# Scaling odd tiles of x on GpSimd, and the modulation products ahead of the weights' low halves, in the first stage of a decoder trunk

## The chip, the core and the metric

One core of a Trainium2 chip runs the whole kernel. The metric is the device time of one execution in microseconds. Two matmul clocks occur on TensorE, 1.2 and 2.4 GHz; the profile gives the granted clock as a share of the higher one. Engines are called TensorE (PE), VectorE (DVE), ScalarE (ACT), GpSimd (POOL) and SyncE (SP, whose queue issues all loads and stores here).

## What is computed

The reference is a trunk of two layers on x (1024 tokens by 1024 channels) with a conditioning vector c: a Mamba-2 layer, then a stick-breaking attention layer over a shared K and V, each with a residual. Only its beginning matters here:

```python
c_act = jax.nn.silu(c)
shift, scale, gate = jnp.split(c_act @ ada_w[i] + ada_b[i], 3, axis=-1)
xf = xf * lax.rsqrt(jnp.mean(xf * xf, axis=-1, keepdims=True) + EPS)
h = (xf * g) * (1.0 + scale) + shift
zxbcdt = h @ in_w
```

So every token (row) of x is divided by its root mean square, every channel is scaled and shifted by numbers that come from a product of a vector (the silu of c) with a matrix (ada_w), and the result h is multiplied by the first projection.

## The kernel before

Matrix products run on float32 values split into a high part and a low part (fp32r): one product is three matmuls (`mm3`, lines 128 to 131: high by high, high weights by low values, low weights by high values).

**The first stage** (lines 158 to 342) is written out by hand: inside `manual_schedule` (line 172) the instructions of TensorE, ScalarE, GpSimd and VectorE run in the order of the code. Loads are issued by SP in the order of lines 179 to 193. Behind the first stage the order of all engines but TensorE in some stages comes from a planner with a simulated timeline (`schedule_with_timeline_sim=True`, line 1107).

The 1024 tokens lie in 8 tiles of 128 tokens by 1024 channels (`xn[t]`), in two halves of 4 tiles (`hf` 0 and 1). The channels are 8 blocks `d` of 128. The steps, each a small function:

- `squares(t)` (200) sums the squares of a tile's rows, on VectorE for t = 1, 3, 7, on ScalarE for the others. `rms(hf)` (214) makes the inverse roots of a half: two steps on ScalarE (139, 140) and three small **root steps** on VectorE (144 to 146).
- `scaled(t)` (217) multiplies a tile by its roots, in place: odd tiles on VectorE (220), even ones on ScalarE (222).
- `turn(d, hf)` (252) transposes block d of the four tiles of a half on TensorE into PSUM (`xp`). `spin` (210) issues filler matmuls whose results are not used.
- `gemv(d)` (224) makes shift and scale of block d: two **modulation products** on VectorE, each a product of a 128x1024 tile of `ada0` (`a`) with the silu of c (`crow`) with an accumulated sum. Line 296 prepares a small vector from the biases for all blocks. `bias(d)` (245) finishes both numbers on ScalarE.
- `split_w(d, V)` (230) splits the weights `ww` of block d: the high halves `wwh` are copied on ScalarE (233), the low halves `wwl` are subtracted on VectorE (234).
- `high(d, hf)` (258) applies scale and shift to `xp` (`hx`, line 260) and copies the high part `h0h` (263), both on ScalarE. `low(d, hf)` (266) subtracts the low part `h0l` on VectorE (268).
- `wave_mm(d, hf)` (270) accumulates three output tiles: nine matmuls, of which the second needs `h0l` and the third `wwl`.

The order is that of lines 280 to 341: squares, roots and scalings of the first half, two transposed blocks, fillers, weights and products of d = 0, then the wave of the first half; then roots and scalings of the second half, its transposes, and so on to d = 7. The loads of later blocks reuse buffers: `a0` has four, `ww` three.

Of the kernel before, what the change touches and what calls it, by code (L numbers as in the profile page):

```python
# [15 lines left out]
ALU = mybir.AluOpType  # L16
# [31 lines left out]
def f(ap):  # L48
    return ap.bitcast(F32)
# [3 lines left out]
def tile_trunk(ctx, tc, xT, xN, c, vec, ada0, adar, wxbc, wwave, wdt, wz, wmo, wk, wv, wq, wqz, wso, out):  # L53
    nc = tc.nc
    V, S, Q, E, Y = nc.vector, nc.scalar, nc.gpsimd, nc.tensor, nc.sync
# [14 lines left out]
    def vv(n, i=None, m=1):  # L70
        o, w = VEC[n]
        if i is None:
            return vt[:, o:o + w]
        return vt[:, o + i:o + i + m]
# [35 lines left out]
    def act_tile(name):  # L110
        return act.tile([P, HT], F32R, tag="a", name=name)

    def mm_tile(name):
        return pmm.tile([P, HT], F32, tag="mm", name=name)
# [43 lines left out]
    with ExitStack() as es:  # L158
# [14 lines left out]
        xn = [px.tile([P, D], F32, name=f"x{t}") for t in range(NC_)]  # L173
# [36 lines left out]
        def spin(x, m):  # L210
            for i in range(m):
                E.matmul(wave[NW - 1][:, HT:], ident, x, start=True, stop=True)
# [4 lines left out]
        def scaled(t):  # L217
            r = rst[:, t // CPH, t % CPH:t % CPH + 1]
            if t % 2:
                V.tensor_scalar(out=xn[t], in0=xn[t], scalar1=r, scalar2=None, op0=ALU.mult)  # L220
            else:
                S.activation(xn[t], xn[t], AF.Identity, scale=r)

        def gemv(d):
            for i, m in enumerate((SH0, SC0)):
                a = a0s[d][:, i, :]
                V.scalar_tensor_tensor(out=a, in0=a, scalar=1.0, in1=crow, op0=ALU.mult, op1=ALU.mult,
                                       accum_out=mod[:, m, d:d + 1])

        def split_w(d, eng):  # L230
            wh = pada.tile([P, NW, P], F32R, tag="wwh", name=f"wwh{d}", bufs=4)
            wl = pada.tile([P, NW, P], F32R, tag="wwl", name=f"wwl{d}", bufs=4)
            S.copy(wh, wws[d])
            eng.tensor_tensor(out=wl, in0=wws[d], in1=f(wh), op=ALU.subtract)
            whl[d] = wh, wl
# [16 lines left out]
        def turn(d, hf):  # L252
            ps = mm_tile(f"xp{d}_{hf}")
            for i in range(CPH):
                E.transpose(ps[:, i * P:(i + 1) * P], xn[hf * CPH + i][:, d * P:(d + 1) * P], ident)
            xps[d, hf] = ps

        def high(d, hf):
            hx = tp.tile([P, HT], F32, tag="hx", name=f"hx0_{d}_{hf}", bufs=3)
            S.activation(hx, xps.pop((d, hf)), AF.Identity, bias=mod[:, SH0, d:d + 1],  # L260
                         scale=mod[:, SC0, d:d + 1])
            h0[d][hf] = (act_tile(f"h0h{d}_{hf}"), act_tile(f"h0l{d}_{hf}"))
            S.copy(h0[d][hf][0], hx)
            hxs[d, hf] = hx

        def low(d, hf):
            hi, lo = h0[d][hf]
            V.tensor_tensor(out=lo, in0=hxs.pop((d, hf)), in1=f(hi), op=ALU.subtract)
# [20 lines left out]
        for t in range(CPH):  # L289
            scaled(t)  # L290
        turn(0, 0)
        turn(1, 0)
        spin(xn[0][:, 0:HT], 3)
        split_w(0, V)
        gemv(0)
        V.scalar_tensor_tensor(out=vv("b_sc0"), in0=vv("b_sc0"), scalar=1.0, in1=vv("g0"), op0=ALU.add,
                               op1=ALU.mult)
        for t in (CPH, CPH + 1):
# [9 lines left out]
        for t in range(CPH, NC_):  # L308
            scaled(t)
        turn(0, 1)  # L310
        split_w(1, V)
        high(0, 1)
        gemv(1)
        low(0, 1)
        bias(1)
        wave_mm(0, 1)
# [327 lines left out]
    with ExitStack() as es:  # L644
# [27 lines left out]
        for hf in range(NH):  # L672
# [3 lines left out]
            for d in range(ND):  # L676
# [4 lines left out]
                for kh in range(2):  # L681
                    wh, wl = load_w(wmo[kh, d], f"o{d}_{hf}_{kh}")
                    for k in range(8):
                        mm3(ps, wh[:, k, :], wl[:, k, :], *yy[kh * 8 + k], kh + k == 0, kh * 8 + k == 15)
                V.scalar_tensor_tensor(out=x1[d][hf], in0=ps, scalar=mod[:, GA0, d:d + 1], in1=xr,
                                       op0=ALU.mult, op1=ALU.add)
# [266 lines left out]
    with ExitStack() as es:  # L953
# [25 lines left out]
        for hf, c0, c1, ds in ((1, 0, 512, (0, 5, 1, 2, 3, 4, 6, 7)), (0, 0, 256, (6, 7, 0, 1, 2, 3, 4, 5)),  # L979
# [10 lines left out]
            for i, d in enumerate(ds):  # L990
                if hf == 0:
                    t = x2t[:, i, :]
                elif d < NPRE:
                    t = x2p[d]
                else:
                    t = pf.tile(sh, F32, tag=f"x2_{d}", name=f"x2_{d}", bufs=1)
# [38 lines left out]
            r = pf.tile(sh, F32, tag="rb", name="rb2_" + n)  # L1035
# [76 lines left out]
```

## Time and profile before

| what | value |
|---|---|
| median of 3 runs | 1459.53 us (1458.59 to 1461.04) |
| the profiled execution | 1462.46 us |
| its span in the trace | 1460.8 us |
| TensorE busy | 1430.3 us, 98% |
| VectorE busy | 962.0 us, 66% |
| ScalarE busy | 736.2 us, 50% |
| GpSimd busy | 516.5 us, 35% |

The span runs from the first to the last instruction of the profiled execution; its time also holds what lies around them. An instruction's row gives its start, its duration, and in brackets the idle time of its engine before it and what ended that. A duration includes time in which an instruction that has been started waits inside the engine. Neighbouring instructions of an engine overlap a little, so the sum of durations is larger than the distance of the starts.

### The profile page before, as it was taken

Reading aid. Unit: us, or ns where it says so; the run is one execution under the profiler, and the core shown is the slowest. Engines: PE = TensorE matmul, PEld = TensorE weight load, DVE = VectorE, ACT = ScalarE, POOL = GpSimd, SP = SyncE. Lnnn points to the kernel's source line nnn. Section 1 sums busy time; section 2 is a strip of 40 time slices with the busy share of each in tenths; the row PEclk is TensorE's granted clock in tenths of the full one; section 3 lists DMA queues with packets and bytes.
Section 4 is the critical chain, followed back from the end, with each engine's and each line's share of the span. In section 5 each row is a group of like instructions: output and inputs, shape, how many; then the busy total and the mean of one; then the engine's idle time right before and its main releaser. Section 6 shows DMA issues by size and latency. Waiting matters only on the chain.

```text
span 1460.8 us, 20961 instructions
## 1 busy us (share of the span) xinstructions
PE 1430.3 (98%) x7772; PEld 1125.7 (77%) x7772; DVE 962.0 (66%) x1211; ACT 736.2 (50%) x1236; POOL 516.5 (35%) x601
## 2 busy tenths in 40 slices
PE   7998999999999999999999999999999999999997
PEld 4777888887777777778888888887777777777797
DVE  5699975455788887975733627516666666667674
ACT  6654533246666666733532424335555555556452
POOL 0021220002555555531011000027666666667531
PEclk9999999999999999999999999999999999999999
DMA  9358875233577766667433546460222122212253
GB/s 368 129 202 318 295 285 182 101 107 132 183 236 220 234 217 217 195 201 266 151 123 128 182 144 227 159 211 31 80 69 70 59 73 63 68 58 81 92 183 116
DMA packets 105446, 235.76 MB, mean 161 GB/s; under 512 B 9344, under 2 KB 40832, under 8 KB 103296
## 3 DMA queue, kind: packets, MB, share of 16 engines
q1 hardware_dynamic: 105344, 234.42, 47.8%
q8 instruction: 61, 1.00, 0.3%
q14 instruction: 41, 0.34, 0.1%
HBM read 188.51 MB, written 45.88 MB: 160 GB/s over the span
## 4 chain that ended last, share of the span: by engine, by line
PE 90%; DVE 5%; ACT 2%; issue 1%; DMA 1%; POOL 0%; SPq 0%; DVEq 0%; ACTq 0%; POOLq 0%
PE av L891 5%; PE pr L129 5%; PE pr L130 5%; PE pr L131 5%; PE sc L838 4%; PE at L870 4%; PE pz L129 4%; PE pz L131 4%; PE pz L130 4%; PE po L131 4%; PE po L130 4%; PE po L129 4%; PE pq L129 2%; PE pqz L129 2%; PE yd L550 2%; PE pq L131 2%
## 5 line engine op out<-in xcount | busy, mean ns | idle before, releaser
L861 POOL TENSOR_TENSOR be<-be,kp 128x1024 f32<-128x1024 f32 (+2 forms) x96 | 163.3, 1702 | 82.6 <-DVE kp L855 73.6
L841 ACT ACTIVATE kp<-sc 128x1024 f32<-128x1024 f32 (+2 forms) x96 | 75.5, 813 | 149.2 <-PE sc L838 111.3
L855 DVE TENSOR_TENSOR_SCAN kp<-kp,pone 128x128 f32<-128x128 f32 (+3 forms) x128 | 96.7, 803 | 63.8 <-POOL kp L848 63.8
L129 PE MATMUL pr<-h0h,hx 128*128 128x512 f32 x336 | 131.7, 392 | 3.8 <-DVE cv L353 3.8
L131 PE MATMUL pr<-h0h,lx 128*128 128x512 f32 x336 | 131.5, 391 | 0.0
L130 PE MATMUL pr<-h0l,hx 128*128 128x512 f32 x336 | 131.5, 391 | 0.0
L129 PE MATMUL pz<-h0h,hz 128*128 128x512 f32 x256 | 113.0, 441 | 0.0
L130 PE MATMUL po<-yl,ho 128*128 128x512 f32 x256 | 100.9, 394 | 0.6 <-DVE yl L664 0.6
L131 PE MATMUL po<-yh,lo 128*128 128x512 f32 x256 | 100.0, 391 | 1.3 <-DVE lo L124 1.3
L131 PE MATMUL pz<-h0h,lz 128*128 128x512 f32 x256 | 100.4, 392 | 0.0
L130 PE MATMUL pz<-h0l,hz 128*128 128x512 f32 x256 | 100.0, 391 | 0.0
L129 PE MATMUL po<-yh,ho 128*128 128x512 f32 x256 | 100.0, 391 | 0.0
L366 POOL TENSOR_TENSOR ar<-ar,crow 128x1024 f32<-128x1024 f32 x12 | 31.1, 2596 | 182.4 <-DMA ar<-adar 163.0
L518 ACT ACTIVATE lm<-lm,nac 128x128 f32<-128x128 f32 x256 | 78.9, 390 | 31.8 <-POOL lm L515 31.8
L855 DVE TENSOR_TENSOR_SCAN kp<-kp,ab,pone 128x512 f32<-128x512 f32 x64 | 78.3, 1265 | 24.7 <-ACT kp L841 14.2
L124 POOL TENSOR_TENSOR lq<-rq,hq 128x256 fp32r<-128x256 f32 x32 | 22.5, 738 | 177.8 <-ACT hq L123 177.8
L515 POOL TENSOR_SCALAR_AFFINE_SELECT lm<-lm 128x1024 f32<-128x1024 f32 x32 | 42.1, 1316 | 118.3 <-DMA lm<-ac_d 108.9
L555 POOL TENSOR_TENSOR sd<-st,eev 128x512 f32<-128x512 f32 x24 | 37.5, 1561 | 126.1 <-ACT st L567 114.2
L353 DVE SCALAR_TENSOR_TENSOR cv<-pr,vt,cv 128x1023 f32<-128x1023 f32 (+2 forms) x63 | 80.2, 1276 | 0.9
L129 PEld LDWEIGHTS pr<-h0h,hx 128*128 128x128 f32 x336 | 63.5, 189 | 17.4 <-issue 4.2
L123 ACT CAST ho<-ro 128x1024 fp32r<-128x1024 f32 x32 | 33.6, 1052 | 84.5 <-PE po L130 74.3
L870 PEld LDWEIGHTS at<-ident,be 128*128 128x128 f32 x576 | 67.2, 140 | 10.6 <-DVE aT L880 0.9
(258 smaller groups left out, 3886.7 us busy)
## 6 DMA issues: line engine op xcount, KB each, us to landing
ar<-adar SPq DMA_DIRECT2D x48, 512.0 KB, 5.3
lm<-ac_d SPq DMA_DIRECT2D x32, 512.0 KB, 5.0
rz<-wz SPq DMA_DIRECT2D x32, 512.0 KB, 3.8
ro<-wmo SPq DMA_DIRECT2D x32, 512.0 KB, 3.7
xs_d<-sv SPq DMA_DIRECT2D x24, 512.0 KB, 4.1
rx<-wxbc SPq DMA_DIRECT2D x21, 512.0 KB, 4.6
a<-ada SPq DMA_DIRECT2D x8, 1024.0 KB, 10.1
xg<-xs_d SPq DMA_DIRECT2D x8, 1024.0 KB, 6.1
```

Of the source, the lines that this page charges most:

```text
L129: E.matmul(ps, wh, xh, start=first, stop=False)
L130: E.matmul(ps, wh, xl, start=False, stop=False)
L131: E.matmul(ps, wl, xh, start=False, stop=last)
L353: V.scalar_tensor_tensor(out=ac[:, i:], in0=ps[:, :T - i], scalar=vv("cw", m * 4 + 3 - i), in1=ac[:, i:], op0=ALU.mult, op1=ALU.add)
L515: Q.affine_select(out=lm, in_=lm, pattern=[[0, HPG], [1, P]], compare_op=ALU.is_ge, fill=-1e30, base=0, channel_multiplier=-1)
L518: e = S.activation(lm[:, h, :], lm[:, h, :], AF.Exp, bias=nac[:, c, h0_ + h:h0_ + h + 1])
L838: E.matmul(ps[:, a, o:o + w], q[hsl[a], x, i * P:(i + 1) * P], kd[hsl[a], y, HT * c:HT * c + w], start=b == 0, stop=b == 2)
L841: S.activation(kp[:, :, ok:ok + w], ps[:, :, o:o + w], AF.Sigmoid, scale=-0.125)
L855: V.tensor_tensor_scan(out=ka, data0=ka, data1=pone.to_broadcast([P, w]), initial=1.0 if top else above[p, i][:, a, 0:1], op0=ALU.mult, op ...
L861: Q.tensor_tensor(out=be[:, :, o:o + w], in0=be[:, :, o:o + w], in1=kp[:, :, ok + 1:ok + w + 1], op=ALU.mult)
L870: E.transpose(ps[:, j, :], be[:, a, j * P:(j + 1) * P], ident)
L891: E.matmul(ps[hsl[a], cs], vd[:, j, hsl[a]], at[j // 4][:, a, j % 4, cs], start=j == 0, stop=j == nj - 1)
```

## The change

Three edits in the first stage. The scaling of odd tiles of x is issued to GpSimd (`Q`) instead of VectorE (`V`). For d = 0 the modulation products stand before the split of the weights instead of behind it. For d = 1 they stand directly behind the transposes of the second half, then comes the high part, and the split of the weights stands behind the high part and before the low part.

```diff
         def scaled(t):
             r = rst[:, t // CPH, t % CPH:t % CPH + 1]
             if t % 2:
-                V.tensor_scalar(out=xn[t], in0=xn[t], scalar1=r, scalar2=None, op0=ALU.mult)
+                Q.tensor_scalar(out=xn[t], in0=xn[t], scalar1=r, scalar2=None, op0=ALU.mult)
             else:
                 S.activation(xn[t], xn[t], AF.Identity, scale=r)
...
         spin(xn[0][:, 0:HT], 3)
+        gemv(0)
         split_w(0, V)
-        gemv(0)
         V.scalar_tensor_tensor(out=vv("b_sc0"), in0=vv("b_sc0"), scalar=1.0, in1=vv("g0"), op0=ALU.add,
                                op1=ALU.mult)
...
         turn(0, 1)
+        gemv(1)
+        high(0, 1)
         split_w(1, V)
-        high(0, 1)
-        gemv(1)
         low(0, 1)
```

## Rows read from the trace of the kernel before

**Rows 1.** Windows: length; busy PE, PEld, DVE, ACT, POOL; clock; DMA share; GB/s.

```profile
29.00:30.00 1.00, 1.00 (x3) 0.82 (x4) 0.00 (x0) 0.97 (x2) 0.00 (x0) 0.68 1.03 428
...
32.00:33.00 1.00, 1.00 (x6) 0.81 (x5) 1.00 (x3) 0.00 (x0) 0.00 (x0) 0.61 1.05 436
...
75.00:115.00 40.00, 36.21 (x162) 28.77 (x161) 39.01 (x41) 21.21 (x25) 8.55 (x3) 1.00 0.61 206
```

**Rows 2.** Chain that ended last, 0 to 40 us: start us, us, what.

```profile
16.14 2.29 DVE a L227 x4
...
28.29 0.61 DVE h0l L268
...
28.94 0.50 PE prw L130
...
31.11 0.43 PE prw L129
...
33.31 0.24 PE prw L130
```

**Rows 3.** Timeline of VectorE, first stage: start us, us, what, [idle before <-releaser].

```profile
12.70 0.16 DVE L146 SCALAR_TENSOR_TENSOR rst<-rtt,rst 128x4 f32<-128x4 f32 x1
12.98 1.42 DVE L220 TENSOR_SCALAR x<-x,rst 128x1024 f32<-128x1024 f32 x2
15.58 0.56 DVE L234 TENSOR_TENSOR wwl<-ww,wwh 128x384 fp32r<-128x384 f32 x1 [1.19 <-ACT wwh L233]
...
18.34 0.16 DVE L296 SCALAR_TENSOR_TENSOR vt<-vt 128x8 f32<-128x8 f32 x1
...
22.62 0.16 DVE L146 SCALAR_TENSOR_TENSOR rst<-rtt,rst 128x4 f32<-128x4 f32 x1
...
42.88 1.22 DVE L227 SCALAR_TENSOR_TENSOR a<-a,crow 128x1024 f32<-128x1024 f32 x1
```

**Rows 4.** Timeline of ScalarE, first stage.

```profile
18.54 0.39 ACT L246 ACTIVATE mod<-mod,vt 128x1 f32<-128x1 f32 x1 [0.91 <-DVE vt L296]
...
24.91 0.49 ACT L233 CAST wwh<-ww 128x384 fp32r<-128x384 f32 x1
26.53 0.78 ACT L260 ACTIVATE hx<-xp,mod 128x512 f32<-128x512 f32 x1 [1.12 <-PE xp L255]
27.34 0.62 ACT L263 CAST h0h<-hx 128x512 fp32r<-128x512 f32 x1
```

**Rows 5.** Timeline of GpSimd, 75 to 420 us.

```profile
82.51 2.84 POOL L366 TENSOR_TENSOR ar<-ar,crow 128x1024 f32<-128x1024 f32 x1 [80.75 <-DMA ar<-adar]
...
122.51 2.41 POOL L366 TENSOR_TENSOR ar<-ar,crow 128x1024 f32<-128x1024 f32 x1 [12.56 <-DVE cv L353]
...
227.90 1.09 POOL L515 TENSOR_SCALAR_AFFINE_SELECT lm<-lm 128x1024 f32<-128x1024 f32 x1 [1.89 <-DMA lm<-ac_d]
```

**Rows 6.** Timelines of VectorE, two stretches after the first stage.

```profile
83.00 3.43 DVE L369 SCALAR_TENSOR_TENSOR ar<-ar,crow 128x1024 f32<-128x1024 f32 x1
...
228.43 1.63 DVE L124 TENSOR_TENSOR lx<-rx,hx 128x1024 fp32r<-128x1024 f32 x1 [2.11 <-ACT hx L123]
```

**Rows 7.** SP: timeline from 10 us, its waits to 60 us, the page's DMA issues.

```profile
12.82 0.33 SPq L188 DMA_DIRECT2D ww<-wwave  x1
...
SPq L188 <- DVE wwl L234: 11.6, 3, 4.7
...
SPq L188 <- DMA a<-ada: 2.2, 1, 2.2
...
a<-ada SPq DMA_DIRECT2D x8, 1024.0 KB, 10.1
```

**Rows 8.** Timeline of TensorE, first stage.

```profile
15.20 1.10 PE L255 MATMUL xp<-ident,x 128*128 128x128 f32 x6 [0.60 <-ACT x L222]
16.09 4.25 PE L212 MATMUL prw<-x,ident 128*128 128x512 f32 x6
...
23.31 2.74 PE L212 MATMUL prw<-x,ident 128*128 128x512 f32 x6
```

## The prediction

> **What bounds the kernel now.** I read the engine rows of the page first, then the windows, the chain of waits of the first 40 us, and the timelines of the engines in that stretch. TensorE is busy nearly all the time, so a stage can be shortened only where TensorE waits or runs at the lower of its two clocks. Both happen in the first stage. There the granted clock falls from 2.4 to 1.2 GHz in 29 to 30 us and is back in 32 to 33 us [rows 1]; before it fell TensorE had stood almost idle from the transposes of the second half of x until the low part h0l came at 28.9. The chain there is: both modulation products on VectorE, then the low part, then TensorE's second matmul at 28.94 [rows 2]. From about 34 us the first stage is a stream of matmuls; then, from 75 to 115, VectorE is busy for 39.0 of 40 us and TensorE for 36.2 [rows 1]: all this starts from the end of the first stage and has no slack that could swallow a later start. So whatever moves in the first 33 us moves the end by about as much.
>
> **The removed work.** Two pairs of scalings leave VectorE, 0.71 us each, 1.42 for two [rows 3]. In the first half VectorE then sat 1.19 us waiting for the high halves wwh, and the products came behind that: VectorE's root steps end at 12.86, its last small product (L296) at 18.50, and ScalarE had waited 0.91 us for it [rows 3, 4]. Without a cost on GpSimd the change would take 0.9 us out of that wait.
>
> **The added work, and its unknown price.** Four TENSOR_SCALAR of 128x1024 come to GpSimd, which is idle from its constants to 82.5 [rows 5], so nothing queues in front of them. No row shows this operation on GpSimd. The one-input row there, the mask of 128x1024, takes 1.09 us; the two-input product of the same size takes 2.41 where nothing disturbs it [rows 5]. VectorE's own 0.71 is the end below [rows 3]. I take t = 1.09, the row with one input and one output of the same shape, and keep 0.71 and 2.41 for the range.
>
> A page makes t larger: the Trainium skill, GPSIMD Engine Reference, section 3.1 (Elementwise — side-by-side cycle accounting), gives about 1.8 cycles of 1.2 GHz per element as the best case for a tight loop, an estimate of 1.54 us for 1024 elements. By it the sum below would be +3.06 us instead of +1.25, a slower kernel; the mask row of this trace, at 1.09, disagrees for one-input work, which is why I leave it to the second rival.
>
> **GpSimd and VectorE exclude each other.** At 82.51 GpSimd's product took 2.84 instead of 2.41, and the VectorE product that came at 83.00 took 3.43 instead of 1.2, ending one ordinary duration after GpSimd's end [rows 5, 6]. It is so for one-input work on GpSimd too: VectorE's subtraction at 228.43 took 1.63, 0.4 more than its 1.2, beside the mask of 227.90, which ended at 228.99 [rows 5, 6]. All these VectorE instructions read two tensors from SBUF, as the products of the modulation (a, crow), the low halves (ww, wwh) and L296 do. So in the changed kernel the scalings and the products do not run beside each other; they take turns. The DMA gives the products no excuse to wait: the first tile of the modulation weights had landed by 12.82, when SP's queue, after a wait of 2.2 us for that landing, issued its next load [rows 7].
>
> **First half, summed.** From 12.86: two products 2.29 [rows 2], two scalings 2t = 2.18, the low halves 0.56, L296 0.16 [rows 3] give 18.05 against 18.50: 0.45 us earlier, whichever of the two engines has the first turn (generally 2t - 2.63). ScalarE's chain from there (bias, high part, square of tile 6, roots) has no other gate that is later, so the second roots, ready at 22.78 [rows 3], come at 22.33. On TensorE the fourth tile of x is now the last: about 17.3 instead of 15.2 for the third (12.86, a product, a scaling, a product, a scaling). Five transposes remain, 0.9 us at the pace of the six of 1.10 [rows 8], and then its three filler matmuls, six records: 2.74 us at full clock (a pitch of 2.6 in all), 4.25 where the clock was low at their beginning [rows 8]. They end at 20.8 to 22.4 instead of 20.34.
>
> **Second half, summed.** From 22.33: 2.29 + 2.18 gives 26.80 for tile 7. One transpose and the hand-over, 0.35 (0.18 by the six, the rest its latency and the hand-over), and the high part starts at 27.15 instead of 26.53 [rows 4]: +0.62. In the old order the low part then waited only for the products (28.29) [rows 2], while the copy of wwh had long been made at 24.91 in ScalarE's idle time [rows 4]. In the new order that copy stands behind the high part on ScalarE, the low halves wait for it on VectorE, and **the low part of x is queued behind them**: 28.58 (the high part took 1.43) + 0.4 for the copy + 0.56 + 0.61 + 0.04 gives 30.2 for the second matmul instead of 28.94. That is +1.25, or 4t - 3.1 for another t: nothing at t = 0.78, over the limit below at t = 1.50, +6.5 at t = 2.41, -0.3 at t = 0.71.
>
> **Then the clock.** The remaining eight matmuls ran at a pitch of 0.43 while the clock was low and would run at 0.24 after [rows 2]. If the clock falls and returns when it did, they end 0.8 us later than now; if it stays low throughout, 1.25 later; if it did not fall at all, 0.3 earlier, for which nothing speaks, since TensorE now does less between 26 and 30 than before. Should the filler matmuls end at 22.4, nine matmuls (2.7), the second filler (2.6) and four transposes follow at 28.35, and the second matmul comes at +2.5. I take **+1.1 us**.
>
> **What I cost at nothing.** The copy of wwh and the bias behind it delay the high part of d = 1, but its low part is there near 31.6, ahead of TensorE's need at 33. On the SP queue the load of the weights ww of d = 4 waits for the low halves of d = 1 (one of three such waits [rows 7]), which come at 29.6 instead of 26.0, and behind it the modulation weights of d = 5 are issued near 30; with a landing time of 10.1 us, the median of that tile [rows 7], they are there by about 40.3, and VectorE takes them up at 42.88 [rows 3]. If that cover were gone, the product would wait on the difference. Earlier products release the buffer of d = 4 earlier, but its issue waited for a landing, not for them.
>
> **Total.** The profiled execution took 1462.46 us, 1.66 more than its span and 2.9 more than the median of the runs. The sum is a difference, so I set it on the median: 1459.5 + 1.1 = 1460.6. A measurement of this kernel can tell about 0.2%, 2.9 us, from no change.
>
> **Rivals.**
> 1. *The overlap works as the edit has it* (GpSimd's scalings hidden beside the products). Against it stand the paired rows above. Even so the first half gains 0.9 at most, and TensorE's fillers, which end at 20.34, take part of that; in the second half tile 7 is ready before the fillers end, the high part starts near 26.2, and the low part still waits for copy and low halves: second matmul near 29.2, +0.3. 1459.8, chance 0.12, no change.
> 2. *The scaling on GpSimd costs far more than the mask.* Its place is tiles 5 and 7 in front of the transposes at 26; its price is 4t - 3.1; it decides from t = 1.50. At 2.41 it gives +6.5, 1466.0; at the middle of 1.5 to 2.41 (+4.7) 1464.2. For it: GpSimd's product, with two inputs, runs at that pace; against it: the mask, with one input as here, does not. Chance 0.20, slower.
> 3. *The planner reorders the stages behind.* Only the first stage is written out by hand on all engines; the order behind it comes from a planned timeline, which moves with this edit. Between 75 and 115 TensorE idles 3.8 of 40 us [rows 1]; an order that removes it gives 1456.8, one that doubles it 1464.4. Chance 0.10 for faster by over 0.2%, 0.07 for slower. Nothing in the profile shows which.
> 4. *The change does not do what it says*, because a tile of modulation weights lands after the roots and the products wait for it: the turns are only swapped and the sum stays; it is inside the forecast.
>
> The forecast itself (turns, t near 1.1, +0.3 to +2.5) has 0.51, rival 1 has 0.12: together 0.63 within 0.2%. Slower: 0.20 + 0.07 = 0.27. Faster 0.10. The range runs from 1457.0, which leaves out most of the planner's gains, to 1465.0, which leaves out t above 2.1.
>
> **What would show it.** Right: GpSimd rows of L220 at 1.1 us undisturbed, up to 2.2 with a turn waited out; products of L227 in the first 28 us at 1.2 to 2.4; bias at about 18.1; tile 7 at about 26.8; the second matmul of the second half near 30.2, waiting on the low part behind the low halves. Wrong: products that stay at 1.22 beside a running scaling (rival 1), a scaling of 1.5 or more with VectorE idle (rival 2), equal first stages with a different later one (rival 3), or a clock that no longer falls at 29.

## The result, and the profile after

The changed kernel took 1467.26 us (median of 4 runs, 1465.74 to 1469.88) against 1459.06 of the kernel before in runs beside it: a ratio of 1.0058 with an interval of 1.0037 to 1.0080, slower by about 8 us. The range ended at 1465.0. The span of the profiled execution is 1467.8 us against 1460.8.

GpSimd's timeline of the changed kernel in the first stage, and below it the summary of its line 220 (durations in ns: least, median, most):

```profile
13.07 7.62 POOL L220 TENSOR_SCALAR x<-x,rst 128x1024 f32<-128x1024 f32 x2 [11.31 <-DVE rst L146]
25.10 7.58 POOL L220 TENSOR_SCALAR x<-x,rst 128x1024 f32<-128x1024 f32 x2 [4.42 <-ACT rst L140]
```

```profile
L220 POOL TENSOR_SCALAR x<-x,rst x4: 2838/3798/4796, 13.1 to 29.8; 128x1024 f32<-128x1024 f32 x4
```

A pair of scalings lasts 7.6 us. The prediction had 1.09 for one; none is under 2.84. The transposes wait for each of them: TensorE took up tile 1 at 17.92 and tile 3 at 20.74, so the first scaling of a pair lasted 4.8 us and the second 2.8.

VectorE's timeline, the answer to [rows 3] and [rows 2]:

```profile
12.86 1.23 DVE L227 SCALAR_TENSOR_TENSOR a<-a,crow 128x1024 f32<-128x1024 f32 x1
...
14.01 1.22 DVE L227 SCALAR_TENSOR_TENSOR a<-a,crow 128x1024 f32<-128x1024 f32 x1
...
15.60 0.94 DVE L234 TENSOR_TENSOR wwl<-ww,wwh 128x384 fp32r<-128x384 f32 x1 [0.36 <-ACT wwh L233]
16.46 0.15 DVE L296 SCALAR_TENSOR_TENSOR vt<-vt 128x8 f32<-128x8 f32 x1
...
34.97 0.56 DVE L234 TENSOR_TENSOR wwl<-ww,wwh 128x384 fp32r<-128x384 f32 x1 [7.74 <-ACT wwh L233]
35.45 0.69 DVE L268 TENSOR_TENSOR h0l<-hx,h0h 128x512 fp32r<-128x512 f32 x1
```

The products follow the root steps directly and keep their 1.2 us: beside them GpSimd bore the whole wait, and VectorE lost only 0.4 us, at the low halves (0.94 for 0.56). L296 is done at 16.6 instead of 18.5, earlier than the prediction had it. ScalarE could use none of that:

```profile
17.57 0.37 ACT L246 ACTIVATE mod<-mod,vt 128x1 f32<-128x1 f32 x1
...
21.31 0.78 ACT L260 ACTIVATE hx<-xp,mod 128x512 f32<-128x512 f32 x1 [3.19 <-PE xp L255]
...
33.10 0.78 ACT L260 ACTIVATE hx<-xp,mod 128x512 f32<-128x512 f32 x1 [5.93 <-PE xp L255]
```

The bias is made at 17.57 (18.54 in [rows 4]), but the high parts now wait 3.19 and 5.93 us for transposes, and start at 21.31 and 33.10 (26.53 in [rows 4]). TensorE's timeline says what the transposes wait for:

```profile
17.92 0.69 PE L255 MATMUL xp<-ident,x 128*128 128x128 f32 x2 [3.41 <-POOL x L220]
20.74 1.33 PE L255 MATMUL xp<-ident,x 128*128 128x128 f32 x5 [2.13 <-POOL x L220]
21.86 4.71 PE L212 MATMUL prw<-x,ident 128*128 128x512 f32 x6
...
31.08 0.49 PE L255 MATMUL xp<-ident,x 128*128 128x128 f32 x3
32.73 0.33 PE L255 MATMUL xp<-ident,x 128*128 128x128 f32 x1 [1.16 <-POOL x L220]
...
36.19 0.80 PE L130 MATMUL prw<-h0l,wwh 128*128 128x512 f32 x1 [1.11 <-DVE h0l L268]
36.78 0.63 PE L131 MATMUL prw<-h0h,wwl 128*128 128x512 f32 x1
...
39.63 0.60 PE L255 MATMUL xp<-ident,x 128*128 128x128 f32 x4
```

Tile 3 comes at 20.74, tile 7 at 32.73, and the second matmul of the second half, which stood at 28.94 in [rows 2], stands at 36.19: +7.25. Its last wait, 1.11 us, is for the low part, which at 35.45 stands behind the low halves of 34.97. The transposes behind that half's nine matmuls start at 39.63. In the kernel before they did so here:

```profile
32.19 0.89 PE L255 MATMUL xp<-ident,x 128*128 128x128 f32 x4
```

That is +7.4 at the end of the part that the change touches, and the median of the runs says +8. The clock (length, busy PE, PEld, DVE, ACT, POOL, clock, DMA, GB/s; the answer to [rows 1]):

```profile
32.00:33.00 1.00, 0.27 (x1) 0.14 (x1) 0.00 (x0) 0.00 (x0) 0.68 (x1) 1.00 1.00 418
...
36.00:40.00 4.00, 3.81 (x13) 3.07 (x13) 3.23 (x6) 1.25 (x3) 0.00 (x0) 0.57 0.36 98
75.00:115.00 40.00, 40.00 (x180) 31.35 (x179) 30.73 (x36) 19.96 (x23) 6.40 (x3) 1.00 0.63 222
```

As before, it falls behind a stretch in which TensorE hardly works, only later (36 to 40 instead of 29 to 33), and the matmuls that follow run at the lower clock (the one of 36.78 lasts 0.63). The window from 75 to 115 now shows work that the kernel before did 7 us earlier, so its row does not compare with that of [rows 1].

### The profile page after: what moved, and what is told of

It is laid out like the page before. It is cut to its first block, busy times and chain, and to the rows that moved or that the text cites. A ratio compares the mean times of both kernels' runs of the same rounds, so it can differ in the third digit from the quotient of the medians.

```text
span 1467.8 us, 20964 instructions
## 1 busy us (share of the span) xinstructions
PE 1430.8 (97%) x7772; PEld 1125.9 (77%) x7772; DVE 956.2 (65%) x1207; ACT 736.2 (50%) x1236; POOL 532.8 (36%) x605
## 4 chain that ended last, share of the span: by engine, by line
PE 89%; DVE 4%; ACT 2%; DMA 1%; issue 1%; POOL 1%; DVEq 0%; SPq 0%; ACTq 0%; POOLq 0%
PE pr L129 5%; PE av L891 5%; PE pr L130 5%; PE pr L131 5%; PE sc L838 4%; PE at L870 4%; PE po L131 4%; PE po L130 4%; PE pz L131 4%; PE po L129 4%; PE pz L129 4%; PE pz L130 4%; PE pq L129 2%; PE pqz L129 2%; PE pq L131 2%; PE yd L550 2%
```

## The experiments

Ratios are against runs of the kernel before on the same chip in the same session; 0.001 is 1.46 us.

**e1: the new order alone.** VectorE scales again; everything else as changed.

```diff
-                Q.tensor_scalar(out=xn[t], in0=xn[t], scalar1=r, ...)
+                V.tensor_scalar(out=xn[t], in0=xn[t], scalar1=r, ...)
```

> The new order of products and low halves stays; the odd tiles are scaled on VectorE again. Price theory (the scaling on GpSimd is long by itself and stands in front of the transposes): nearly all of the +8 us is gone; in the first half the bias comes near 17.6 (0.9 earlier), in the second the low part still stands behind copy and low halves, second matmul near 29.4 against 28.94; end between -0.5 and +1 us of before. Order theory (the low part queued behind the low halves is what costs): at least +3 us stay, second matmul after 32.

Measured: 1460.74 us, ratio 1.0011 (1.0002 to 1.0021). The bias at 17.69, and on TensorE:

```profile
29.27 0.80 PE L130 MATMUL prw<-h0l,wwh 128*128 128x512 f32 x1 [1.11 <-DVE h0l L268]
...
32.60 0.60 PE L255 MATMUL xp<-ident,x 128*128 128x128 f32 x4
```

The order costs 0.3 us at the second matmul, 0.4 at the transposes behind, and about 1.6 at the end, a little more than was expected. That is the price theory's outcome; the order theory asked for at least 3 us, and for the second matmul after 32.

**e2: GpSimd alone,** in the old order (only the first edit of the diff).

> The odd tiles are scaled on GpSimd, the order is the old one. Price theory: about +7 us against before, 0.7 to 1.0 less than the whole change (the low part then waits for nothing but the high part). Order theory: below +4 us. Turns theory (a scaling is 4.8 us only because VectorE's products hold it up, 2.8 undisturbed): here VectorE has no product until the low halves are made, so the first scaling of each half should last 2.8 and the second, beside the products, up to 4.8; the sum of the two stays 7.6.

Measured: 1463.79 us, ratio 1.0034 (1.0021 to 1.0047), +5 us. GpSimd's line, one product of VectorE beside the second scaling, and TensorE's second matmul with the transposes behind it:

```profile
L220 POOL TENSOR_SCALAR x<-x,rst x4: 2845/3426/4032, 13.2 to 27.3; 128x1024 f32<-128x1024 f32 x4
```

```profile
17.34 2.05 DVE L227 SCALAR_TENSOR_TENSOR a<-a,crow 128x1024 f32<-128x1024 f32 x1
```

```profile
33.92 0.50 PE L130 MATMUL prw<-h0l,wwh 128*128 128x512 f32 x1 [0.23 <-DVE h0l L268]
...
36.55 1.05 PE L255 MATMUL xp<-ident,x 128*128 128x128 f32 x4
```

The end moves by 2 us less than the price theory expected. With VectorE all but idle a scaling takes 2.85; beside the products it takes 4.03 and one of the products 2.05. So the scaling is long by itself, and the waits of the two engines for each other come on top: beside two products they are 2.0 us together, all of it on GpSimd in the whole change (4.8 less 2.84), here 1.2 on GpSimd and 0.8 on VectorE. The sum of two scalings is 6.9, not the 7.6 that was expected. The whole change is 3.5 us worse by the ratios than GpSimd alone (the intervals overlap); by the rows the second matmul is 2.3 earlier here, since the new order puts both products beside the first scaling (tile 7 at 31.34 here, 32.73 there) and the low part behind the low halves.

**e3: a product of two tensors on GpSimd** instead of a scaling by a scalar operand.

```diff
-                Q.tensor_scalar(out=xn[t], in0=xn[t], scalar1=r, scalar2=None, op0=ALU.mult)
+                Q.tensor_tensor(out=xn[t], in0=xn[t], in1=r.to_broadcast([P, D]), op=ALU.mult)
```

> As the whole change, but GpSimd multiplies by the root broadcast along the row as a second tensor input instead of by a scalar operand. Price theory with the rows of before: 2.4 us undisturbed instead of 2.8, so about 0.8 us less per half, end near +6.5 instead of +8; if the broadcast input costs nothing to read it could fall to 1.1 each, end near +2. If the scalar operand is not the cost at all, the duration stays at 2.8.

Measured: 1464.94 us, ratio 1.0040 (1.0026 to 1.0053), +5.8.

```profile
L220 POOL TENSOR_TENSOR x<-x,rst x4: 2754/2839/2870, 13.0 to 26.3; 128x1024 f32<-128x1024 f32 x4
```

```profile
13.04 5.64 POOL L220 TENSOR_TENSOR x<-x,rst 128x1024 f32<-128x1024 f32 x2 [11.28 <-DVE rst L146]
```

```profile
14.02 2.90 DVE L227 SCALAR_TENSOR_TENSOR a<-a,crow 128x1024 f32<-128x1024 f32 x1
...
16.86 2.23 DVE L234 TENSOR_TENSOR wwl<-ww,wwh 128x384 fp32r<-128x384 f32 x1
```

```profile
33.15 0.51 PE L130 MATMUL prw<-h0l,wwh 128*128 128x512 f32 x1 [1.11 <-DVE h0l L268]
...
35.13 0.60 PE L255 MATMUL xp<-ident,x 128*128 128x128 f32 x4
```

A pair takes 5.6 instead of 7.6, each 2.75 to 2.87 with a wait for VectorE's turn inside. This is the turn-taking that the prediction described: product, GpSimd, product (2.90), GpSimd, low halves (2.23). From 16.86, where VectorE's second product gives way, to the end of the pair at 18.68 are 1.8 us: an estimate of what one of these costs without the wait, 1.0 less than the scaling. The pair is 2.0 shorter where 0.8 was expected, and the second matmul comes at 33.15, 3.0 earlier than in the whole change.

**e4: a constant factor.**

```diff
-                Q.tensor_scalar(out=xn[t], in0=xn[t], scalar1=r, scalar2=None, op0=ALU.mult)
+                Q.tensor_scalar(out=xn[t], in0=xn[t], scalar1=1.0, scalar2=None, op0=ALU.mult)
```

> As the whole change, but the factor on GpSimd is the constant 1.0 instead of the root of each row: the odd tiles stay unscaled, nothing else changes. Pointer theory (the scalar per partition read from memory makes it long): about 1.1 us undisturbed, end near +2 us. Price theory without the pointer (this operation on GpSimd is long whatever its scalar): 2.8 us as in the whole change, end near +8.

```profile
L220 POOL TENSOR_SCALAR x<-x x4: 2767/2769/2772, 9.8 to 21.6; 128x1024 f32<-128x1024 f32 x4
```

2.77 us each: the scalar per partition is not the cost, the pointer theory falls. The end (1460.85 us, ratio 1.0006, 0.9995 to 1.0017) says nothing for or against: without the roots GpSimd starts at 9.8, long before the transposes. The expectation overlooked that.

This run also shows how a scaling and VectorE get on beside each other. GpSimd's rows, then VectorE's:

```profile
9.82 5.50 POOL L220 TENSOR_SCALAR x<-x 128x1024 f32<-128x1024 f32 x2 [8.07 <-PE prw L212]
18.86 5.50 POOL L220 TENSOR_SCALAR x<-x 128x1024 f32<-128x1024 f32 x2 [3.53 <-ACT sq L207]
```

```profile
12.63 0.98 DVE L144 SCALAR_TENSOR_TENSOR rtt<-rst 128x4 f32<-128x4 f32 x1 [0.69 <-ACT rst L140]
...
18.96 2.01 DVE L204 SCALAR_TENSOR_TENSOR sq<-x 128x1024 f32<-128x1024 f32 x1 [1.61 <-DMA x<-xN]
...
22.96 1.22 DVE L227 SCALAR_TENSOR_TENSOR a<-a,crow 128x1024 f32<-128x1024 f32 x1
```

The scalings start at 9.82, 12.55, 18.86 and 21.59. VectorE's root step at 12.63 lasts 0.98 us instead of 0.16 and its sum of squares at 18.96 lasts 2.01 instead of 1.23: both are held until about 0.9 us after the start of a scaling. The product at 22.96 comes 1.4 us after such a start and keeps its 1.22, and the scaling beside it keeps its 2.77. So these instructions of VectorE are shut out at the beginning of a scaling only: an estimate, from these rows, of 0.9 us of the 2.77. The low halves of the whole change agree: with its own 2.84 the first scaling, over at 17.9, began at about 15.05, and the low halves of 15.60 were held for 0.4, until about 15.98.

**e10: a copy.** GpSimd copies the odd tiles onto themselves (`Q.tensor_copy(xn[t], xn[t])`).

> As the whole change, but GpSimd copies the odd tiles onto themselves instead of scaling them: they stay unscaled. Only the duration is of use. If one input and one output of this size are what the mask's 1.09 us stands for, the copy takes 1.0 to 1.2; if the mask is the exception and every elementwise operation on GpSimd has its own price, nothing says which, up to the 2.8 of the scaling.

```profile
L220 POOL COPY x<-x x4: 1036/1041/1444, 9.3 to 20.4; 128x1024 f32<-128x1024 f32 x4
```

A copy takes 1.04 us. One input, one output and 1024 elements cost about 1.0 to 1.1 us for a copy, as for the mask of [rows 5]; for the multiplication they cost 2.77. The price hangs on the operation.

**e5: the blocks needed next on VectorE.** Of each odd tile VectorE scales columns 0 to 255, GpSimd the rest.

```diff
-                Q.tensor_scalar(out=xn[t], in0=xn[t], scalar1=r, ...)
+                V.tensor_scalar(out=xn[t][:, 0:2 * P], in0=xn[t][:, 0:2 * P], scalar1=r, ...)
+                Q.tensor_scalar(out=xn[t][:, 2 * P:], in0=xn[t][:, 2 * P:], scalar1=r, ...)
```

> The new order stays. Of each odd tile VectorE scales the first 256 columns, the two blocks that the next transposes read, and GpSimd the other 768. Price theory (GpSimd's scaling costs because the transposes of block 0 and 1 stand behind it): the scaling leaves the path; second matmul of the second half near 29.3 as with VectorE alone, end within 1.5 us of before, against +8 for the whole change. If its mere presence costs (products and low halves held up by the exclusion): at least +3 stays. The duration for 768 columns tells a price per element from a fixed one: 2.1 us undisturbed if it is all per element, 2.8 if it is fixed.

Measured: 1459.49 us, ratio 0.9999 (0.9990 to 1.0007).

```profile
L221 POOL TENSOR_SCALAR x<-x,rst x4: 2304/2791/3602, 13.2 to 24.5; 128x768 f32<-128x768 f32 x4
```

```profile
25.52 0.60 PE L256 MATMUL xp<-ident,x 128*128 128x128 f32 x4
...
29.25 0.51 PE L130 MATMUL prw<-h0l,wwh 128*128 128x512 f32 x1 [1.11 <-DVE h0l L269]
```

GpSimd is still busy 5.5 to 6 us in each half, and it costs nothing: the transposes no longer wait for it, and the second matmul stands where VectorE alone had it in e1. The least of the four, 2.30 us for 768 columns against 2.84 for 1024, is a price mostly per element (2.1 ns each and 0.7 us fixed, if the two points lie on a line).

**e8 and e9: half the dose.** Tiles 1 and 3 on GpSimd and 5 and 7 on VectorE (`if t % 2 and t < CPH`), and the reverse.

> The whole change, with tiles 1 and 3 on GpSimd and 5 and 7 on VectorE. Price theory: the second roots come 2.2 late as in the whole change, the second half then adds 0.4 for the order alone: second matmul near 31.5, end about +3 us. If only the second half matters for the end (its transposes come after fillers that hide the first): within 1 us of before.

> The whole change, with tiles 5 and 7 on GpSimd and 1 and 3 on VectorE: the complement of e8. If the two halves add up (8.2 - 5.4): about +2.8 us. If each hides behind the other (in the whole change the fillers behind the late first half end at 31.1 and tile 7 comes at 32.7, so the second half adds only 1.6 there): second roots at 22.0 as with VectorE alone, two scalings 7.6, tile 7 at 29.6, second matmul near 33.1 (+4.1), end +4 to +5.

Measured: e8 1465.06 us, ratio 1.0037 (1.0024 to 1.0050), +5.4; e9 1464.62 us, ratio 1.0032 (1.0020 to 1.0045), +4.7. TensorE in e8, then in e9:

```profile
20.82 1.33 PE L257 MATMUL xp<-ident,x 128*128 128x128 f32 x5 [2.13 <-POOL x L220]
21.94 3.54 PE L212 MATMUL prw<-x,ident 128*128 128x512 f32 x6
...
29.98 0.60 PE L257 MATMUL xp<-ident,x 128*128 128x128 f32 x4
...
33.71 0.76 PE L130 MATMUL prw<-h0l,wwh 128*128 128x512 f32 x1 [1.11 <-DVE h0l L270]
```

```profile
29.82 0.33 PE L257 MATMUL xp<-ident,x 128*128 128x128 f32 x1 [2.38 <-POOL x L220]
...
33.28 0.80 PE L130 MATMUL prw<-h0l,wwh 128*128 128x512 f32 x1 [0.81 <-DVE h0l L270]
```

e8 is 2.4 us worse than expected. The expectation carried the late roots forward and left out TensorE's own queue: behind tile 3 (20.82) come five transposes, the first fillers, partly at the low clock, nine matmuls and the second fillers, without a gap up to the transposes of the second half at 29.98, while tile 7 is there at 26.4. In e9 it is tile 7 that is late (29.82), as expected. In the whole change both are: the fillers end at 31.1 and tile 7 comes at 32.7. So the halves do not add up: at the second matmul they make 4.8 and 4.3, the whole change 7.25, and each stands partly in the shadow of the other. The times (5.4 and 4.7 against 8.5) go the same way, but their intervals are too wide to show it.

**e6, e7, e11, e12: what is to be had here without GpSimd.** In e6 VectorE scales, and the split of the weights of block 1 stands ahead of the high part again:

```diff
         turn(0, 1)
         gemv(1)
+        split_w(1, V)
         high(0, 1)
-        split_w(1, V)
         low(0, 1)
```

> Scaling on VectorE; in the second half the split of the weights of block 1 stands ahead of the high part again, so the low part waits for the high part only, and the products still follow the roots directly. From the run with the new order on VectorE: the low part comes 0.9 earlier, second matmul near 28.3 instead of 29.3 (28.94 in the kernel before). End 0.5 to 1.5 us below that run and 0 to 1 us below before: hardly to be told from it by the time, but by the row.

```profile
28.42 0.50 PE L130 MATMUL prw<-h0l,wwh 128*128 128x512 f32 x1 [0.23 <-DVE h0l L268]
...
31.51 1.05 PE L255 MATMUL xp<-ident,x 128*128 128x128 f32 x4
```

The second matmul at 28.42, 0.85 earlier than in e1: that is the price of the low part behind copy and low halves. The end does not tell it: 1459.40 us, ratio 1.0001 (0.9990 to 1.0011).

e7 adds to e6 one filler (`spin(xn[0][:, 0:HT], 1)`) behind `turn(0, 1)`; e12 adds it to the kernel before; e11 is e7 with two fillers ahead of those transposes and two behind, instead of three and one.

> As e6, and one more filler matmul behind the transposes of the second half, in time in which TensorE waits. If the fall of the clock at 29 us is owed to TensorE's idle time from 26 to 28, it should not come, and the eight matmuls that ran at 0.43 run at 0.24: 1.5 us more, the end near -2 us against before. If the filler is in the way or the clock falls all the same: end as in e6.

> As e7, with one filler taken from in front of the transposes of the second half and put behind them (2 and 2 instead of 3 and 1). If the fillers in front hold the transposes (they end at 25.4 and tile 6 is there at 24.1): second matmul 0.85 earlier than in e7, near 27.4, the clock stays up, end 0.8 us below e7, near -2.7 against before. If the roots or the products bound it instead: as e7.

> The kernel before, with one more filler matmul behind the transposes of the second half and nothing else. If e7's gain is the clock's: no fall at 29, the eight matmuls at 0.24, about -1.5 us. If it is the order's: as before.

Measured: e7 1457.19 us, ratio 0.9987 (0.9978 to 0.9995); e11 1456.40 us, ratio 0.9976 (0.9967 to 0.9985); e12 1458.45 us, ratio 0.9994 (0.9985 to 1.0003). The window of e7 and of e12 in which the clock fell before [rows 1], and TensorE's rows of e11:

```profile
29.00:30.00 1.00, 1.00 (x6) 0.80 (x5) 0.52 (x1) 0.86 (x2) 0.00 (x0) 1.00 0.98 410
```

```profile
29.00:30.00 1.00, 0.96 (x4) 0.82 (x5) 0.00 (x0) 0.95 (x2) 0.00 (x0) 1.00 1.02 421
```

```profile
24.57 0.60 PE L255 MATMUL xp<-ident,x 128*128 128x128 f32 x4
...
27.41 0.50 PE L130 MATMUL prw<-h0l,wwh 128*128 128x512 f32 x1 [0.23 <-DVE h0l L268]
...
29.39 0.60 PE L255 MATMUL xp<-ident,x 128*128 128x128 f32 x4
```

In both profiles the clock stays at 2.4 GHz (1.00, in the windows behind as well) and the transposes behind come at 30.26 and 31.02, 1.9 and 1.2 earlier than before. e12 alone is not to be told from no change by the runs. e11 brings the second matmul to 27.41 and those transposes to 29.39, 2.8 earlier; it is faster than the kernel before by 3.5 us, with an interval of 2.2 to 4.8.

**All kernels together.** The start of the transposes behind the second half's nine matmuls in the one profiled execution of each, the difference to 32.19, and the ratio's difference in us:

| kernel | start, us | against before | end, us (interval) |
|---|---|---|---|
| whole change | 39.63 | +7.4 | +8.5 (5.4 to 11.7) |
| e8 tiles 1, 3 | 37.23 | +5.0 | +5.4 (3.5 to 7.3) |
| e9 tiles 5, 7 | 36.85 | +4.7 | +4.7 (2.9 to 6.6) |
| e2 GpSimd alone | 36.55 | +4.4 | +5.0 (3.1 to 6.9) |
| e3 two inputs | 35.13 | +2.9 | +5.8 (3.8 to 7.7) |
| e1 order alone | 32.60 | +0.4 | +1.6 (0.3 to 3.1) |
| e5 head on VectorE | 32.18 | 0.0 | -0.1 (-1.5 to 1.0) |
| e6 | 31.51 | -0.7 | +0.1 (-1.5 to 1.6) |
| e12 | 31.02 | -1.2 | -0.9 (-2.2 to 0.4) |
| e7 | 30.26 | -1.9 | -1.9 (-3.2 to -0.7) |
| e11 | 29.39 | -2.8 | -3.5 (-4.8 to -2.2) |

What moves in the first stage moves the end one for one within the intervals, with one exception: e3. In its profiled execution the clock did not fall behind the late second half; whether its other executions were less lucky, one profile cannot show, and it stays open.

## Why the prediction was wrong

- **What bounds, and that the first stage reaches the end one for one: right** (the table).
- **The price of the scaling: wrong, and this is the step that failed.** "I take t = 1.09, the row with one input and one output of the same shape, and keep 0.71 and 2.41 for the range." Measured: 2.84 with VectorE idle, 2.77 with a constant factor. A copy costs 1.04, so the mask's row was a good row for a copy and no row for a multiplication. The upper end was wrong as well: the row of the two-input product, 2.41, was taken as the dearest thing GpSimd could do at this size. The range followed from it ("to 1465.0, which leaves out t above 2.1"). With t = 2.84 the prediction's own formula, 4t - 3.1, gives +8.3; measured are +7.25 at that matmul and +8 at the end. That the formula comes so near is in part luck: it leads the first half through the bias and would bring the second roots at 25.8; they came at 24.9, by way of the transposes of tile 3. The mechanism, scalings in front of the transposes, was that of rival 2; its chance was put at 0.20.
- The Trainium skill, GPSIMD Engine Reference, section 3.1, by which the prediction estimated 1.54 us, was nearer than the mask's row and still only about half of what the scaling takes here. The Trainium skill, GPSIMD Engine Reference, section 4.1 (Engine selection), calls one-input work on GpSimd roughly line-rate. Against the 0.71 us of VectorE's scaling [rows 3] the copy (1.04) takes 1.5 times as long and agrees roughly; the scaling by a scalar (2.84) takes 4 times as long and does not.
- **The exclusion: right in the sum of the whole change, wrong as a rule.** Products and scalings do cost each other time (4.8 against 2.84; 2.05 and 2.90 against 1.2). The first half's sum holds with the real price: 12.86 + 2.29 + 2 x 2.84 gives 20.83 for tile 3, measured about 20.7, since the first scaling waited for both products. But "they take turns" for their whole length held for GpSimd's two-input product (e3) alone. A scaling shuts VectorE out for about 0.9 us at its beginning, and a product that comes later runs beside it at no cost to either (e4). That is the sign that the prediction gave for rival 1, though not rival 1's time, since the scaling's own price stays in front of the transposes. The prediction's own row hinted at it: the subtraction of 228.43 lost 0.4 us beside a mask that ran on for 0.56. So L296 came at 16.6, not 18.05, and the early bias was worth nothing.
- **"ScalarE's chain from there has no other gate that is later": wrong,** as a consequence of t: the transposes of tile 3 are the later gate, by 3.19 us.
- **The low part queued behind copy and low halves: right in kind.** It costs 0.85 (e1 against e6); the prediction's terms for copy and low halves, 0.4 and 0.56, make 0.96.
- **TensorE's queue behind a late tile 3** was in the prediction as the upper case (+2.5); with the real price it became the rule and alone carries e8.
- **The clock: right.** It fell again, behind the new idle stretch, and no run in which TensorE idled longer kept it up but e3's profile. The profiles of e7 and e12 show that the fall belongs to that idle time: with one filler in it, it does not come.
- **The costs put at nothing held.** The loads behind SP's longer wait were in time: VectorE idles before no product of the first stage after 30 us. The row of 42.88 that the prediction set against them is the product of block 4, not 5 as it said; the block 5 product comes at 48.58, so the cover was larger than stated.
- **The planner (rival 3) did nothing:** behind the first stage every engine runs the same instructions in the same order in the traces of both kernels, and the shift at the end of the touched part (+7.4) agrees with the one at the end of the kernel.

## What to carry to other kernels

The price of an operation on another engine is that operation's own: the number of inputs and the shape do not give it (copy 1.04, mask 1.09, product 2.41, scaling 2.8 on the same 128x1024 tile), and where no row has it, the upper end must lie above the dearest row. When work goes to a slower engine, ask first which part of it the next reader needs: a quarter of the tile kept on the fast engine took all of the 8 us away. And a wait of TensorE that cannot be removed can still be filled, so that the matmuls behind it run at full clock.

## What the runs showed of the hardware that was not expected

- GpSimd's multiplication by a scalar (2.77 to 2.85 us for 128x1024) is longer than its product of two tensors of that size (2.41 in [rows 5]; an estimate of 1.8 in e3, where the second input is one number per row) and 2.7 times its copy (1.04). Why was not tried.
- A scaling that finds VectorE in its two-input products waits for them (it grew by 1.9 us in the whole change); once it has begun, it holds VectorE up for about 0.9 us and then runs beside it (e4). GpSimd's two-input product held VectorE's product nearly to its own end (2.90 us for 1.22, e3). Why the two differ is open.
